# Hi/lo products of 384, 256 and 320 columns instead of three of 320, with a fold in PSUM, in a decoder layer on one core

## The chip, the cores and the metric

The kernel runs on one core of one Trainium2 chip. The metric is the device time of one execution in microseconds. Before the change it is 2016.62 us, the median of 3 runs (2016.05 to 2017.05). The numbers below come from one profiled execution of the kernel before, which took 2011.32 us itself.

## The reference

One decoder layer, 2048 channels wide, in float32, for a prompt of 256 tokens and for 8 sequences of 8 new tokens, which share all weights. Each token group has its own conditioning vector. Cut to what matters:

```python
mod = jax.nn.silu(c) @ w_ada + b_ada                    # six shifts, scales and gates
h = _rmsnorm(x, norm1_g) * (1 + sc1) + sh1
p = h @ w_in                                            # q, k, v, og, u, ga, gb, alr
o, s_new = _gla(q, k, v, loga, s0)                      # gated linear attention, 4 heads
y_a = _rmsnorm(o, gla_norm_g) * jax.nn.silu(og)
y_b = _pool(u_ext, pos0, w_pool, pool_scale)            # (window mean - u) @ w_pool, times a scale
merged = jax.nn.sigmoid(ga) * y_a + jax.nn.sigmoid(gb) * y_b
x = x + g1 * (merged @ w_o)
h2 = _rmsnorm(x, norm2_g) * (1 + sc2) + sh2
gate, up = jnp.split(h2 @ w_gu, 2, axis=-1)             # 2 x 5632 columns
x = x + g2 * ((jax.nn.silu(gate) * up) @ w_down)
y = _rmsnorm(x, final_norm_g)
```

Outputs are the normalised tokens of both groups and the new attention and pooling states.

## The kernel before, in words

Tokens are columns. Both groups lie side by side in tiles of T = 320 columns (256 of the prompt, 64 of the new tokens), with 128 channels on the partitions. So a projection has a piece of weights, 128 input by 128 output channels, as the stationary operand and 320 token columns as the moving one, and adds its result into one bank of PSUM.

Float32 accuracy is had from a split into a high and a low part in the type fp32r. Activations are split once when they are made: `hh` and `hl` (input of w_in), `mh` and `ml` (of w_o), `h2h` and `h2l` (gate and up), `ah` and `al` (down), `dh` and `dl` (of w_pool). Weights are split as they arrive: SyncE starts a transfer into a `raw` tile, ScalarE casts 512 columns of it to `whi` (L152), and VectorE subtracts to get `wlo` (L153); `whi` and `wlo` have five buffers each, and one holds two contraction tiles of 256 output channels. `mm3` (L165 to L168) then issues three products into the same columns of the bank: whi by high, whi by low, wlo by high. These three are called a triple in the following.

A unit is 256 output channels: a tile `ps` with two banks ([128, 2, 512], of which 320 columns in each are used), filled by all contraction tiles of the unit, each with two triples, one a bank. There are two `ps` buffers. When the unit is done, ScalarE or VectorE takes its result out (`evac`, the activation of gate, the product of up, or `residual`), and the buffer goes to the unit after the next.

The stages follow each other. In the head of the kernel the conditioning is worked out while w_in's first group of units runs in slices of the contraction: 2, 2, 4, 4 and 4 of the 16 contraction tiles, 15 units each time, with the partial results added in SBUF. In slices of two tiles a unit has only 12 products. Then come the units of heads 1 to 3 with all 16 tiles (96 products), between which the steps of the attention and pooling are taken from a queue; w_o in 8 units; the second norm; and the FFN in two parts, each of 22 units of gate and up and 8 units of down with 22 contraction tiles (132 products). Down's units end with `residual` (L999), as do w_o's.

What sets the order: the program is written engine by engine by a scheduler that simulates the work by estimated times; SyncE's weight transfers in the head are held in the written order. Each engine takes its instructions strictly in its own order, and waits on semaphores for the others. `xT`, the transposed input, lies in the tiles that later hold the low parts (tag `hl`), and is spilled to DRAM by POOL (L499) before these are written.

## Time and profile before

| | before |
|---|---|
| median of 3 runs | 2016.62 us (2016.05 to 2017.05) |
| profiled execution | 2011.32 us, span 2009.5 us |
| mean granted TensorE clock | 0.989 |
| matmuls, and weight loads | 15008 each |
| HBM read, written | 373.96 MB, 24.67 MB; 198 GB/s over the span |

The page gives for each engine its busy time, its share of the span, and its instructions. PE is TensorE's products and PEld its weight loads, which run beside them. A row of the groups reads: line, engine, operation, output tile <- input tiles, shapes, count; then busy us and mean ns of one; then the idle time of the engine just before, and what ended it. A shape such as 128*128 128x320 is a stationary operand of 128 rows by 128 columns and a moving one of 320 columns. A row of the timeline begins with the start and the length in us. A row of the waits reads: who waited, for whom, us in total, times, longest us. A row of the windows gives the length of the stretch, busy us and count of PE, PEld, VectorE, ScalarE and POOL, the granted clock, the transfers' busy share and GB/s.

### The profile page before, as it was taken

What the parts mean: (1) busy time and instruction counts of PE and PEld (TensorE: products, weight loads), DVE (VectorE), ACT (ScalarE), POOL (GpSimd) and SP (SyncE); (2) the same over time, 40 slices, a digit from 0 to 9 for tenths busy, and PEclk for the clock granted to TensorE, in tenths of its full rate; (3) what the DMA queues carried; (4) which work ended last, traced back from release to release, by engine and by line L of the source; (5) the groups of instructions that cost most, each with busy time, mean ns of one, the idle gap of its engine ahead of it and who ended that gap; (6) DMA issues with size and microseconds to landing.
All of it is one profiled execution on the core that took longest, in us unless ns stands there. A gap on an engine that the chain in (4) does not pass through costs nothing.

```text
span 2009.5 us, 37187 instructions
## 1 busy us (share of the span) xinstructions
PE 1956.2 (97%) x15008; PEld 1848.8 (92%) x15008; DVE 1015.5 (51%) x1881; ACT 820.1 (41%) x1466; POOL 141.8 (7%) x261
## 2 busy tenths in 40 slices
PE   7999999999999999999989999999999999999997
PEld 5789998888899899889979999999999999999997
DVE  3555665465546433665574444444444444444554
ACT  4333374354336333643344333343333344344443
POOL 1112220111001100110020000000000000000000
PEclk9999999999999999999989999999999999999998
DMA  9888754775975887569737666544444544444442
GB/s 301 285 302 272 234 155 147 253 255 186 314 237 167 281 263 229 156 230 340 234 105 223 206 205 203 168 148 154 145 152 149 155 149 147 151 154 144 150 142 91
DMA packets 319598, 400.83 MB, mean 199 GB/s; under 512 B 13529, under 2 KB 259801, under 8 KB 319089
## 3 DMA queue, kind: packets, MB, share of 16 engines
q1 hardware_dynamic: 307154, 358.21, 55.8%
q0 software_dynamic: 12272, 40.25, 5.7%
q8 instruction: 117, 1.92, 0.4%
q14 instruction: 55, 0.45, 0.1%
HBM read 373.96 MB, written 24.67 MB: 198 GB/s over the span
## 4 chain that ended last, share of the span: by engine, by line
PE 91%; DMA 5%; DVE 1%; ACT 1%; issue 1%; SPq 0%; POOL 0%; ACTq 0%; POOLq 0%; DVEq 0%
PE ps L166 27%; PE ps L168 26%; PE ps L167 26%; PE pm L218 5%; DMA raw<-w_in 2%; DMA raw<-w_ada 2%; PE pm L129 2%; PE pm L800 1%; PE pm L769 1%; PE pm L821 1%; DMA xn<-x_sample 1%; DVE wlo L153 0%; PE pm L796 0%; PE pm L758 0%; PE pm L641 0%
## 5 line engine op out<-in xcount | busy, mean ns | idle before, releaser
L153 DVE TENSOR_TENSOR wlo<-raw,whi 128x512 fp32r<-128x512 f32 x952 | 659.6, 697 | 834.0 <-ACT whi L152 827.2
L152 ACT CAST whi<-raw 128x512 fp32r<-128x512 f32 x952 | 587.0, 621 | 1013.4 <-PE ps L167 878.0
L166 PE MATMUL ps<-hh,whi 128*128 128x320 f32 x1408 | 445.9, 317 | 7.3 <-ACT whi L152 3.1
L166 PE MATMUL ps<-h2h,whi 128*128 128x320 f32 x1408 | 437.8, 311 | 5.1 <-ACT h2h L1042 5.1
L168 PE MATMUL ps<-hh,wlo 128*128 128x320 f32 x1408 | 441.6, 314 | 0.2 <-DVE wlo L153 0.2
L167 PE MATMUL ps<-hl,whi 128*128 128x320 f32 x1408 | 440.3, 313 | 0.3 <-DVE hl L495 0.3
L167 PE MATMUL ps<-h2l,whi 128*128 128x320 f32 x1408 | 435.5, 309 | 0.0
L168 PE MATMUL ps<-h2h,wlo 128*128 128x320 f32 x1408 | 435.5, 309 | 0.0
L166 PEld LDWEIGHTS ps<-hh,whi 128*128 128x128 f32 x1408 | 266.6, 189 | 30.8 <-issue 15.8
L168 PEld LDWEIGHTS ps<-hh,wlo 128*128 128x128 f32 x1408 | 266.6, 189 | 8.1 <-issue 6.1
L166 PEld LDWEIGHTS ps<-h2h,whi 128*128 128x128 f32 x1408 | 265.0, 188 | 9.3 <-ACT h2h L1042 6.1
L167 PEld LDWEIGHTS ps<-hl,whi 128*128 128x128 f32 x1408 | 266.9, 190 | 7.0 <-issue 5.4
L167 PEld LDWEIGHTS ps<-h2l,whi 128*128 128x128 f32 x1408 | 264.9, 188 | 0.0
L168 PEld LDWEIGHTS ps<-h2h,wlo 128*128 128x128 f32 x1408 | 264.9, 188 | 0.0
L166 PE MATMUL ps<-ah,whi 128*128 128x320 f32 x704 | 218.7, 311 | 0.0
L168 PE MATMUL ps<-ah,wlo 128*128 128x320 f32 x704 | 217.5, 309 | 0.0
L167 PE MATMUL ps<-al,whi 128*128 128x320 f32 x704 | 217.5, 309 | 0.0
L167 PEld LDWEIGHTS ps<-al,whi 128*128 128x128 f32 x704 | 132.2, 188 | 0.0
L166 PEld LDWEIGHTS ps<-ah,whi 128*128 128x128 f32 x704 | 132.2, 188 | 0.0
L168 PEld LDWEIGHTS ps<-ah,wlo 128*128 128x128 f32 x704 | 132.2, 188 | 0.0
L218 PE MATMUL pm<-raw,scT 128*32 128x128 f32 (+1 forms) x2688 | 109.9, 295 | 8.1 <-DMA raw<-w_ada 8.0
L218 PEld LDWEIGHTS pm<-raw,scT 128*32 128x32 f32 x2688 | 69.1, 111 | 36.0 <-issue 19.5
(279 smaller groups left out, 1542.6 us busy)
## 6 DMA issues: line engine op xcount, KB each, us to landing
raw<-w_ada SPq DMA_DIRECT2D x192, 512.0 KB, 5.8
raw<-w_gu SPq DMA_DIRECT2D x176, 512.0 KB, 3.5
raw<-w_in SPq DMA_DIRECT2D x173, 512.0 KB, 3.9
raw<-w_down SPq DMA_DIRECT2D x80, 512.0 KB, 3.3
S<-state_gla POOLq DMA_DIRECT2D x16, 1024.0 KB, 8.2
o_gs<-S POOLq DMA_DIRECT2D x16, 1024.0 KB, 5.9
raw<-w_o SPq DMA_DIRECT2D x32, 512.0 KB, 4.7
raw<-w_down SPq DMA_DIRECT2D x16, 256.0 KB, 2.6
```

Source lines behind the costliest of these rows:

```text
L129: PE.transpose(out, in_, ident[:k, :k])
L152: S.copy(hi, raw)
L153: V.tensor_sub(lo, raw, hi.bitcast(F32))
L166: PE.matmul(ps, lhsT=whi, rhs=xhi, start=start, stop=False)
L167: PE.matmul(ps, lhsT=whi, rhs=xlo, start=False, stop=False)
L168: PE.matmul(ps, lhsT=wlo, rhs=xhi, start=False, stop=stop)
L218: ins = PE.matmul(ps[32 * j:32 * j + 32, 0:w], lhsT=scT[:, k, :], rhs=raws[j], start=k == 0, stop=k == KT - 1, tile_position=(0, 32 * j))
L769: PE.matmul(pt, lhsT=E["kdn"][:, s, d * P:(d + 1) * P], rhs=E["vn"][:, s], start=s == 0, stop=s == 1)
L800: PE.matmul(pt[32 * j:32 * j + 32, :], lhsT=qeP[:, d, 4 * gg + j, :], rhs=E["S0", gg, d][:, j], start=False, stop=d == 1, tile_position=(0 ...
L821: PE.matmul(pt, lhsT=kpz[:, gg, j, d * P:(d + 1) * P], rhs=E["vp"][:, gg], start=True, stop=True)
```

## The change

High and low part of an activation now lie in one tile of 640 columns (`hx`, `mx`, `h2x`, `ax`, `dx`): 0 to 320 high, 320 to 640 low. A triple still covers 960 columns in three products, cut in other places (`EX` = 64):

- h: whi by columns 0 to 384, so all of the high part and the first 64 columns of the low part, into columns 0 to 384 of the bank;
- m: whi by columns 384 to 640, the other 256 of the low part, into columns 64 to 320;
- l: wlo by columns 0 to 320, as before, into columns 0 to 320.

What the first 64 low columns gave lies in columns 320 to 384 of the bank and belongs into 0 to 64. `fold` does this once a `ps` tile, before it is taken out: ScalarE copies the 64 columns of both banks to SBUF (one buffer), VectorE adds them into the bank. There are 180 such tiles: 75 in the head, 29 in heads 1 to 3, 8 of w_o, 44 of gate and up, 16 of down, and 8 of w_pool.

In the FFN's second part the products stand in another order: gate and up issue h, h, m, m, l, l over the two banks, down h, l, m for each bank. The padding tile `rpad` shrinks from 120 to 88 columns. `xT` now lies in the tile of both parts, so the high part too is written only after POOL's spill.

```diff
+EX = 64
-    rp.tile([P, 120], F32, name="rpad")
+    rp.tile([P, 88], F32, name="rpad")
...
-    def mm3(ps, whi, wlo, xhi, xlo, start, stop):
-        PE.matmul(ps, lhsT=whi, rhs=xhi, start=start, stop=False)
-        PE.matmul(ps, lhsT=whi, rhs=xlo, start=False, stop=False)
-        PE.matmul(ps, lhsT=wlo, rhs=xhi, start=False, stop=stop)
+    def halves(x):
+        return x[..., 0:T], x[..., T:2 * T]
+
+    def mm_pair(banks, ws, x, start, stop, order="hml"):
+        for part in order:
+            for ps, (whi, wlo) in zip(banks, ws):
+                if part == "h":
+                    PE.matmul(ps[:, 0:T + EX], lhsT=whi, rhs=x[:, 0:T + EX], start=start, stop=False)
+                else:
+                    o, w, rhs = (EX, whi, x[:, T + EX:2 * T]) if part == "m" else (0, wlo, x[:, 0:T])
+                    PE.matmul(ps[:, o:T], lhsT=w, rhs=rhs, start=False, stop=stop and part == order[-1])
+
+    def mm3(ps, whi, wlo, x, start, stop):
+        mm_pair([ps], [(whi, wlo)], x, start, stop)
+
+    def fold(ps):
+        t = wp.tile([P, 2, EX], F32, tag="fold", bufs=1, name=nm("fold"))
+        S.copy(t, ps[:, :, T:T + EX])
+        V.tensor_tensor(ps[:, :, 0:EX], ps[:, :, 0:EX], t, op=ALU.add)
+        return ps
...
-                for i in range(2):
-                    mm3(ps[:, i, :T], whi[:, i * P:(i + 1) * P], wlo[:, i * P:(i + 1) * P],
-                        xh[kt], xl[kt], kt == k0, kt == k1 - 1)
+                jobs = [(ps[:, i], (whi[:, i * P:(i + 1) * P], wlo[:, i * P:(i + 1) * P])) for i in range(2)]
+                for part in ([jobs] if both else [[b] for b in jobs]):
+                    mm_pair([b for b, _ in part], [w2 for _, w2 in part], x[kt], kt == k0, kt == k1 - 1, order)
             ada_pump()
-        return ps
+        return fold(ps)
...
-                xT.append(hp.tile([P, T], F32, tag="hl%d" % k, name="xT%d" % k))
+                xT.append(hp.tile([P, 2 * T], F32, tag="hx%d" % k, name="xT%d" % k)[:, 0:T])
...
-                pg = proj(wgu, f * P, 0, KT, h2h, h2l)
+                pg = proj(wgu, f * P, 0, KT, h2x, both=pi == 1)
...
-            ps = proj(wdn, 256 * ui, f0, f1, ah, al)
+            ps = proj(wdn, 256 * ui, f0, f1, ax, "hlm" if pi == 1 else "hml")
```

How this stands in the engines' orders is shown at three places. In a row stand the line, the operation, output <- inputs with their buffer numbers, and the shape of the moving operand or of the output.

TensorE, the down product of FFN part 2, before: the triple of one contraction tile in the second bank, and the next contraction tile's in the first bank (`ah` and `al` are the activations, `whi` and `wlo` the weights).

```order
L166 MATMUL ps_21143<-ah_18462,whi_21248 128x320
L167 MATMUL ps_21143<-al_18463,whi_21248 128x320
L168 MATMUL ps_21143<-ah_18462,wlo_21249 128x320
L166 MATMUL ps_21143<-ah_18743,whi_21264 128x320
L167 MATMUL ps_21143<-al_18744,whi_21264 128x320
L168 MATMUL ps_21143<-ah_18743,wlo_21265 128x320
```

The same place now, and below it two contraction tiles of gate and up in part 2, where "x2" is the same form twice, once for each bank:

```order
L176 MATMUL ps_21606<-ax_18885,whi_21711 128x384
L179 MATMUL ps_21606<-ax_18885,wlo_21712 128x320
L179 MATMUL ps_21606<-ax_18885,whi_21711 128x256
L176 MATMUL ps_21606<-ax_19171,whi_21727 128x384
L179 MATMUL ps_21606<-ax_19171,wlo_21728 128x320
L179 MATMUL ps_21606<-ax_19171,whi_21727 128x256
```

```order
L176 MATMUL ps_16887<-h2x_11666,whi_16974 128x384 x2
L179 MATMUL ps_16887<-h2x_11666,whi_16974 128x256 x2
L179 MATMUL ps_16887<-h2x_11666,wlo_16975 128x320 x2
L176 MATMUL ps_16887<-h2x_11667,whi_16974 128x384 x2
L179 MATMUL ps_16887<-h2x_11667,whi_16974 128x256 x2
L179 MATMUL ps_16887<-h2x_11667,wlo_16975 128x320 x2
```

The number of products is the same; their widths are 384, 320 and 256 or come in pairs over the banks.

VectorE in the head's first slice, before: subtractions for coming weights and the evacuations that fall to it.

```order
L153 TENSOR_TENSOR wlo_528<-raw_525,whi_527 128x512
L351 TENSOR_SCALAR v_281<-ps_460 128x640
L153 TENSOR_TENSOR wlo_532<-raw_525,whi_531 128x512
L340 COPY u_282<-ps_478 128x8x8 x2
L153 TENSOR_TENSOR wlo_586<-raw_583,whi_585 128x512
```

The same units on VectorE now:

```order
L188 TENSOR_TENSOR ps_376<-ps_376,fold_395 128x2x64
L188 TENSOR_TENSOR ps_399<-ps_399,fold_418 128x2x64
L188 TENSOR_TENSOR ps_436<-ps_436,fold_449 128x2x64
L154 TENSOR_TENSOR wlo_527<-raw_524,whi_526 128x512
L154 TENSOR_TENSOR wlo_531<-raw_524,whi_530 128x512
L188 TENSOR_TENSOR ps_453<-ps_453,fold_466 128x2x64
L371 TENSOR_SCALAR v_265<-ps_453 128x640
L188 TENSOR_TENSOR ps_474<-ps_474,fold_493 128x2x64
L360 COPY u_266<-ps_474 128x8x8 x2
```

VectorE now has an addition for every unit, also for those that ScalarE takes out, ahead of the coming weights' subtractions.

ScalarE in the same slice, before: casts of weights and its evacuations of q, k, the first half of v, and u.

```order
L152 CAST whi_481<-raw_479 128x512
L349 ACTIVATE q_279<-ps_392 128x640
L349 ACTIVATE k_280<-ps_412 128x640
L349 ACTIVATE v_281<-ps_446 128x640
L152 CAST whi_527<-raw_525 128x512
L152 CAST whi_531<-raw_525 128x512
L338 COPY u_282<-ps_478 128x2x256
```

The same now:

```order
L153 CAST whi_477<-raw_475 128x512
L187 COPY fold_395<-ps_376 128x128
L369 ACTIVATE q_263<-ps_376 128x640
L187 COPY fold_418<-ps_399 128x128
L369 ACTIVATE k_264<-ps_399 128x640
L187 COPY fold_449<-ps_436 128x128
L153 CAST whi_526<-raw_524 128x512
L153 CAST whi_530<-raw_524 128x512
L369 ACTIVATE v_265<-ps_436 128x640
L187 COPY fold_466<-ps_453 128x128
```

Each evacuation has a copy in front of it, and between the two lies VectorE's addition; the third unit's copy stands before two casts and its evacuation behind them. Over the whole program VectorE's order grows by the 180 additions, and ScalarE's by the 180 copies; SyncE has 708 transfers in both, some of w_ada, w_in and w_o in another order.

More of the change, by code (lines that the diff above doesn't have):

```diff
@@ L293, in s3 @@
         return ap.rearrange("p (b t) -> p b t", t=LS)
-    hh = [hp.tile([P, T], F32R, tag="hh%d" % k, name="hh%d" % k) for k in range(KT)]
-    hl = [None] * KT
+    hx = [None] * KT
     def hilo(hi, lo, x):
@@ L976, in body @@
     pump(len(queue))
[L979 to L980 removed]
+    mx = [hp.tile([P, 2 * T], F32R, tag="hx%d" % k, name="mx%d" % k) for k in range(KT)]
     for k in range(KT):
[L982 removed]
+        hilo(*halves(mx[k]), merged[k // 4][:, k % 4])
     mix.close()
@@ L1033, in body @@
     rs = rstd_bcast(acc)
-    h2h = [hp.tile([P, T], F32R, tag="hh%d" % k, name="h2h%d" % k) for k in range(KT)]
-    h2l = [hp.tile([P, T], F32R, tag="hl%d" % k, name="h2l%d" % k) for k in range(KT)]
+    h2x = [hp.tile([P, 2 * T], F32R, tag="hx%d" % k, name="h2x%d" % k) for k in range(KT)]
+    h2h, h2l = zip(*(halves(x) for x in h2x))
     for k in range(KT):
```

67 lines of the change are left out of this document (31 added, 36 removed).

## The prediction

> **What bounds the kernel now.** I read the page first (busy shares, then the chain that ended last), after it the groups by form, the matmuls' pitch in the timeline, and the list of waits.
>
> ```profile
> span 2009.5 us, 37187 instructions
> PE 1956.2 (97%) x15008; PEld 1848.8 (92%) x15008; DVE 1015.5 (51%) x1881; ACT 820.1 (41%) x1466; POOL 141.8 (7%) x261
> PE 91%; DMA 5%; DVE 1%; ACT 1%; issue 1%; SPq 0%; POOL 0%; ACTq 0%; POOLq 0%; DVEq 0%
> ```
>
> TensorE is busy for 97% of the span and carries 91% of the chain; VectorE (51%) and ScalarE (41%) have room. The work that the change reshapes is these groups, the first product of each three:
>
> ```profile
> L166 PE MATMUL ps<-hh,whi 128*128 128x320 f32 x1408 | 445.9, 317 | 7.3 <-ACT whi L152 3.1 <-ACT hh L491 2.7 <-DVE mg L927 0.6
> L166 PE MATMUL ps<-h2h,whi 128*128 128x320 f32 x1408 | 437.8, 311 | 5.1 <-ACT h2h L1042 5.1
> L166 PE MATMUL ps<-ah,whi 128*128 128x320 f32 x704 | 218.7, 311 | 0.0
> L166 PE MATMUL ps<-mh,whi 128*128 128x320 f32 x256 | 79.8, 313 | 0.0
> L166 PE MATMUL psy<-dh,whi 128*128 128x320 f32 x32 | 10.7, 336 | 3.4 <-ACT q L349 3.4
> ```
>
> 1408 + 1408 + 704 + 256 + 32 = 3808 triples. The 311 to 336 ns is the length of one, which overlaps its neighbours. What counts is the distance between starts:
>
> ```profile
> 1500.00:1600.00 100.00, 100.00 (x684) 100.00 (x683) 45.04 (x73) 38.36 (x62) 0.00 (x0) 1.00 0.48 150
> 1500.09 0.31 PE L166 MATMUL ps<-ah,whi 128*128 128x320 f32 x1
> 1500.23 0.31 PE L167 MATMUL ps<-al,whi 128*128 128x320 f32 x1
> 1500.38 0.31 PE L168 MATMUL ps<-ah,wlo 128*128 128x320 f32 x1
> 1500.53 0.31 PE L166 MATMUL ps<-ah,whi 128*128 128x320 f32 x1
> ```
>
> The first row is a stretch of 100 us in FFN part 1: 684 products, nothing idle, clock 1.00, so 100/684 = 0.146 us each and 0.44 us a triple, the same within a triple and from one to the next (0.14, 0.15, 0.15). 3808 x 0.44 = 1676 us of the span are these triples: 1 ns on a triple is 3.8 us. That decides the sign.
>
> **The triple: 384 + 256 + 320 columns for three of 320.** The sum stays 960 columns, the products three, the weight loads three. If a product costs so much a column and so much fixed, nothing moves. Other widths of the same kind are in the trace:
>
> ```profile
> 894.04 0.39 PE L821 MATMUL pm<-vp,kpz 128*128 128x512 f32 x1
> 894.27 0.31 PE L168 MATMUL psy<-dh,wlo 128*128 128x320 f32 x1
> 435.00 0.77 PE L640 MATMUL pm<-cumr,w 128*128 128x272 f32 x4
> 435.60 0.31 PE L166 MATMUL ps<-hh,whi 128*128 128x320 f32 x1
> L640 PE MATMUL pm<-cumr,w 128*128 128x400 f32 x8 | 3.1, 401 | 0.0
> L640 PE MATMUL pm<-cumr,w 128*128 128x272 f32 x8 | 2.6, 325 | 0.7 <-ACT w L627 0.7
> ```
>
> 512 columns hold TensorE 0.23 us, 320 hold it 0.146: 0.084/192 = 0.44 ns a column and 6 ns fixed by the rounded numbers; with 0.227, which rounds to the same 0.23, it is 0.417 ns a column and 13 ns fixed. On any such straight line a triple costs 0.44 us as before. The four products of L640 are 272, 400, 272 and 400 columns (the line's two forms, below them in the rows, as often as each other): 0.60 us, where the line gives 1344 x 0.417 + 4 x 13 = 613 ns. Uneven widths were thus not dearer here, but 13 ns cheaper for two pairs, with 10 ns of rounding. I take 0, by the straight line through the two widths with many rows; ends: -6.5 ns a triple (half of 13, a triple has one uneven pair) = -25 us, and the load's bound below for the other.
>
> **The weight load under 256 columns.** Each product needs a new load of 128 columns, which runs beside the product before it. The shortest cover falls from 320 columns (0.146) to 256, which the line puts at 0.120.
>
> ```profile
> L218 PEld LDWEIGHTS pm<-raw,scT 128*32 128x32 f32 x2688 | 69.1, 111 | 36.0 <-issue 19.5 <-DMA raw<-w_ada 11.3 <-DMA x<-xspill 0.4
> L512 PEld LDWEIGHTS pm<-hh,wal 128*64 128x64 f32 x16 | 2.2, 135 | 0.2
> L166 PEld LDWEIGHTS ps<-h2h,whi 128*128 128x128 f32 x1408 | 265.0, 188 | 9.3 <-ACT h2h L1042 6.1 <-issue 3.0 <-ACT h2h L1041 0.2
> ```
>
> From 64 to 128 columns a load grows by 53 ns, 0.83 a column, so 106 ns of the 188 is the part that grows and the rest passes in the pipe: an estimate that fits under 0.120. A second bound: in the 0.60 us of L640, the two products of 400 columns need at least 2 x 400 x 0.417 = 333 ns, which leaves at most 267 ns for the two of 272, 0.133 each, with loads of 128 columns under them. So a load never held TensorE longer than 133 ns there, and the 256-column product can be stretched by 13 ns at most: 3808 x 13 = +50 us. I take 0 here: 106 is nearer to what two sizes of load show. The Trainium skill ("TensorE: Matmul & The Clock Gate", section LDWEIGHTS) has a load take its columns over 1.2 ns, 107 ns for 128; the rows above agree by their slope. By that rule the sum is the same as by the rows, with 13 ns to spare; a load that also needed the fixed 13 ns to itself would just use it up.
>
> **Product orders in FFN part 2.** h, h, m, m, l, l over two banks, and h, l, m in the down product: no product more or less. In before, a product that reuses the weights' tile (L166 to L167), one that changes it (L167 to L168) and one that changes the bank (L168 to L166) all start 0.14 to 0.15 apart, so the order is worth 0.
>
> **The fold.** Columns 320 to 384 of a bank have to come back to 0 to 64: one ScalarE copy of 128 elements a partition out of PSUM and one VectorE add into it, per ps tile, 180 times, ahead of the evacuation.
>
> ```profile
> L1089 ACT COPY yn<-pm 128x128 f32<-128x128 f32 x16 | 4.2, 265 | 8.1 <-PE pm L129 8.1
> L1089 DVE COPY yn<-pm 128x128 f32<-128x128 f32 x16 | 4.7, 292 | 3.6 <-ACT yn L1089 3.5
> L1002 DVE TENSOR_TENSOR rt<-ps,mod 128x64 f32<-128x64 f32 x48 | 10.3, 215 | 0.0
> ```
>
> The copy is 0.27; the add of 128 elements lies between 0.22 (64 elements) and something over 0.29 (a copy of 128), I take 0.30; with a hand-over between engines of 0.05 at most (40.26 to 40.31 in the rows below) the chain is 0.6 us. 180 x 0.27 = 49 us more on ScalarE, 180 x 0.30 = 54 on VectorE: 869 and 1070 us of 2010, under 54%, so as work it is hidden under TensorE. What is not hidden is the delay of the evacuation, where TensorE waits for the bank. There are two ps buffers; a unit of 14 us and more (96 products and more at 0.146) covers it entirely: all FFN, w_o and the units of heads 1 to 3. It is short in the head's two slices of two contraction tiles, 30 units of 12 products (12 x 0.146 = 1.76 us). A unit's last product ends 0.3 after its start, the evacuation takes 0.7 to 0.8, and the buffer is wanted 13 x 0.146 = 1.9 after that start: cover 0.75, left after the fold about 0.15. But the units don't all begin evacuating at once:
>
> ```profile
> 39.56 0.70 ACT L349 ACTIVATE q<-ps 128x640 f32<-128x640 f32 x1 [3.36 <-PE ps L168]
> 40.31 0.41 PE L166 MATMUL ps<-hh,whi 128*128 128x320 f32 x1
> 115.74 0.82 DVE L347 SCALAR_TENSOR_TENSOR q<-ps,q 128x640 f32<-128x640 f32 x1
> 116.61 0.41 PE L166 MATMUL ps<-hh,whi 128*128 128x320 f32 x1 [0.22 <-DVE q L347]
> ```
>
> Here 40.31 follows the end of its evacuation (40.26) by 0.05, and 116.61 its own (116.56) by 0.05. These are the first and the last of ten such places among the 30 where less than 0.6 lies between; their mean is 0.25, so ten times 0.35 = +3.5 us. Ends: 0, since this stretch also waits for weights, and 30 x 0.6 = +18, if every unit pays in full.
>
> ```profile
> 0.00:200.00 200.00, 183.87 (x1519) 157.45 (x1520) 102.10 (x196) 70.49 (x129) 32.59 (x71) 0.99 0.87 290
> ACT whi L152 <- DMA raw<-w_in: 78.5, 21, 8.2
> PE psy L166 <- ACT q L349: 3.4, 1, 3.4
> PE ps L166 <- DVE mg L927: 0.6, 1, 0.6
> ```
>
> In the first 200 us the transfers are busy 0.87 of the time, and ScalarE waits 78.5 us for w_in: a late bank there can hide behind a late weight. In heads 1 to 3 two places wait for an evacuation or its follower (last two rows): 2 x 0.55 = +1.1, ends 0 and +1.2. The last two places are the ends of w_o and of the kernel, where the residual stands alone on the path:
>
> ```profile
> 1027.64 0.31 PE L168 MATMUL ps<-mh,wlo 128*128 128x320 f32 x1
> 1027.99 0.48 DVE L999 SCALAR_TENSOR_TENSOR x<-ps,mod,x 128x256 f32<-128x256 f32 x1 [0.56 <-PE ps L168]
> 1031.63 1.41 PE L1025 MATMUL pm<-acc,cst 128*128 128x320 f32 x2 [3.68 <-DVE acc L996]
> 1993.36 0.31 PE L168 MATMUL ps<-ah,wlo 128*128 128x320 f32 x1
> 1993.70 0.48 DVE L999 SCALAR_TENSOR_TENSOR x<-ps,mod,x 128x256 f32<-128x256 f32 x1 [7.60 <-PE ps L168]
> ```
>
> In both the fold stands between the last product and the first residual: +0.6 each; ends 0.3 and 0.6, the lower if the copy, whose columns only the h products write, starts under the last two products (2 x 0.146). In before, the first residual at 1027.99 reads only bank 0, complete three products earlier, and yet begins after the last product: so waits here are for the whole tile, and I take 0.6. The Trainium skill ("PSUM — Partial Sum Buffer", section PSUM bank collisions raise a hardware error) wants an engine kept off a bank that TensorE still writes; by that too the new orders buy nothing here and the sum is the same.
>
> Both added instructions also stand in queues. VectorE's add waits for the copy, and behind it on VectorE wait the wlo halves of coming weights; ScalarE's copy waits for the unit's last product, and behind it the whi halves. The five whi and wlo buffers hold ten contraction tiles of 6 x 0.146 = 0.88 us, so TensorE has up to 8.8 us in hand where the transfers are on time: 0, with the 18 above as its bound. The high part, now in the low part's tile, waits like it for POOL's spill of xT:
>
> ```profile
> L499 POOL DMA_DIRECT2D xspill<-xT x16: 542/542/622, 35.3 to 167.3; - x16
> 64.72 0.51 ACT L490 ACTIVATE hh<-xh,mod 128x256 fp32r<-128x256 f32 x1
> ```
>
> The first spills are issued from 35.3, the high parts that come into their tiles are written from 64.72: 29 us cover it, cost 0. SyncE has the same 708 transfers with a few swapped in order: 0, since TensorE's waits for them are in the head only.
>
> **Sum.** Triple 0, load 0, order 0, head +3.5, heads 1 to 3 +1.1, ends of w_o and kernel +1.2: +5.8 us on the profiled run's 2011.32 (span 2009.5). The median of the runs shown, 2016.62, lies 5.3 us above that run; the same difference on it gives **2022.4 us**, 0.29% slower. A measurement of this kernel can tell about 0.2%, 4.0 us, from no change.
>
> **The rivals.** (a) Faster: the uneven triple is cheaper. For it: the 13 ns of L640; against it: the rounding, and the straight line. Half of it, 3 ns a triple, gives -11.4 + 5.8 = -5.6: 2011.0. It decides from (4.0 + 5.8)/3808 = 2.6 ns a triple on; at 6.5 ns it is 2016.6 - 24.7 + 5.8 = 1997.7. (b) Slower by the load: it isn't covered by 256 columns and costs up to 13 ns a triple, 2016.6 + 5.8 + 50 = 2072; half of that, 2047. Against it: the slope of 0.83 ns a column. (c) Slower by the queues: every unit of the two short slices pays the whole fold and 18 us come in place of 3.5: 2037. For it: in-order queues with one fold buffer; against it: 20 of 30 units have the room, and the waits for weights hide part. (d) No change: the folds are all hidden or pressed under a measurement's uncertainty (the head's 3.5 gone behind weights): 2016.6 + 2.3 = 2019.
>
> **Chances.** The forecast with its folds' costs between 4 and 13: 0.43. (a) 0.27. (b) 0.09. (c) 0.06. (d) 0.15. So faster 0.27, same 0.15, slower 0.58. The range goes from 1998, the 6.5 ns end of (a), to 2037, the end of (c), and leaves out (b) and little of (a), 0.13 in all; the likeliest case's own range is 2020 to 2030.
>
> **What would show it.** In a dense stretch of the FFN a triple still takes 0.44 us, with 0.173, 0.120 and 0.146 for the three widths; a 256-column product at 0.13 would be (b), a triple under 0.437 (a). In the two short slices, waits of TensorE for ScalarE's or VectorE's evacuation grow by 2 to 5 us in sum; at the end of w_o the residual starts 0.9 after the last product instead of 0.35. I am wrong if the FFN's time per unit moves at all.

## The result, and the profile after

The changed kernel takes 2041.7 us (median of 4 runs, 2038.11 to 2042.34) against 2016.53 us of the kernel before in the same comparison: a ratio of 1.0121, 95% interval 1.0104 to 1.0139. It is slower by 25 us, where 6 were forecast. The profiled execution took 2038.11 us.

The page after, busy shares and the chain that ended last:

```profile
span 2036.3 us, 37600 instructions
PE 1965.3 (97%) x15008; PEld 1858.2 (91%) x15008; DVE 1061.3 (52%) x2061; ACT 852.0 (42%) x1645; POOL 137.4 (7%) x261
PE 87%; DMA 6%; DVE 3%; ACT 2%; issue 1%; POOL 0%; SPq 0%; ACTq 0%; DVEq 0%; POOLq 0%
```

The span is 26.8 us longer, and TensorE is busy for only 9 of them. The added work is no larger than forecast (VectorE +46 us where 54 were forecast, ScalarE +32 for 49), but VectorE and ScalarE have come into the chain: 3% and 2%, 1% each before.

To find where the time went, I compare when each stage's first product starts in the two traces. The stretches follow each other without a gap, so the differences add up to the span's, but for rounding:

| stretch | before, us | after, us | difference |
|---|---|---|---|
| up to w_in's first product | 34.6 | 35.8 | +1.2 |
| head, five slices of w_in | 266.2 | 283.6 | +17.4 |
| heads 1 to 3 | 597.6 | 600.4 | +2.8 |
| w_o and second norm | 139.8 | 138.2 | -1.6 |
| FFN part 1, gate and up | 331.2 | 333.6 | +2.3 |
| FFN part 1, down | 154.9 | 154.9 | 0.0 |
| FFN part 2, gate and up | 309.8 | 312.1 | +2.3 |
| FFN part 2, down | 159.3 | 160.4 | +1.1 |
| from the last product's start | 16.1 | 17.5 | +1.4 |

The head's row is the distance between these two products of the timeline, w_in's first and the first of head 1, before:

```profile
34.58 0.42 PE L166 MATMUL ps<-hh,whi 128*128 128x320 f32 x1 [2.68 <-ACT hh L491]
...
300.78 0.31 PE L166 MATMUL ps<-hh,whi 128*128 128x320 f32 x1
```

and after:

```profile
35.75 0.66 PE L176 MATMUL ps<-hx,whi 128*128 128x384 f32 x1 [3.48 <-DVE hx L514]
...
319.31 0.34 PE L176 MATMUL ps<-hx,whi 128*128 128x384 f32 x1
```

Of the head's 17.4 us, 9.7 are lost in the 30 units of the two-tile slices (w_in's first product to the first of the third slice: 74.5 us before, 84.2 after) and 7.7 in the 45 units of the four-tile slices: 3.4 in the first two of these, 4.2 in the last. The waits from 34 to 122 us, which take in the two-tile slices, show how. TensorE's waits for evacuations before:

```profile
PE ps L166 <- DVE v L351: 0.3, 1, 0.3
PE ps L166 <- DVE q L347: 0.2, 1, 0.2
```

and after, the three longest, with the waits of ScalarE and VectorE for the fold:

```profile
PE ps L176 <- DVE mg L367: 3.6, 3, 2.2
PE ps L176 <- DVE mg L371: 2.1, 2, 1.6
PE ps L176 <- DVE k L367: 2.0, 1, 2.0
...
ACT fold L187 <- PE ps L179: 32.2, 16, 3.7
DVE ps L188 <- ACT fold L187: 20.2, 13, 3.3
```

TensorE now waits 9.7 us for evacuations, three smaller rows included, which in this stretch of before cost it 0.5 us; for the weights' high halves it waits less than before (1.1 us instead of 3.1), and for low halves not at all, as before. ScalarE stands 32 us in front of fold copies whose unit isn't done, VectorE 20 us in front of additions whose copy isn't done; what is behind them in the two queues stands too. One such place in the timeline. The unit whose buffer is wanted ends with the product at 76.92, the next unit, in the other buffer, with the one at 78.67; the product at 82.00 gets the first one's buffer:

```profile
76.92 0.31 PE L179 MATMUL ps<-hx,wlo 128*128 128x320 f32 x1
78.67 0.31 PE L179 MATMUL ps<-hx,wlo 128*128 128x320 f32 x1
79.44 0.62 ACT L153 CAST whi<-raw 128x512 fp32r<-128x512 f32 x1 [3.84 <-DMA raw<-w_in]
79.97 0.26 ACT L187 COPY fold<-ps 128x128 f32<-128x128 f32 x1
80.09 0.69 DVE L154 TENSOR_TENSOR wlo<-raw,whi 128x512 fp32r<-128x512 f32 x1 [3.30 <-ACT whi L153]
80.70 0.29 DVE L188 TENSOR_TENSOR ps<-ps,fold 128x128 f32<-128x128 f32 x1
81.03 0.82 DVE L367 SCALAR_TENSOR_TENSOR k<-ps,k 128x640 f32<-128x640 f32 x1
82.00 0.42 PE L176 MATMUL ps<-hx,whi 128*128 128x384 f32 x1 [2.02 <-DVE k L367]
```

ScalarE had waited 3.84 us for a transfer of weights when the cast began at 79.44; both units' copies stand behind that cast, the second unit's not until 81.08; the first addition comes behind the subtraction that needs the cast, though its copy ended at 80.23, and the evacuation behind the addition. It ends at 81.85, 4.9 us after its unit's last product, and TensorE has waited 2.02 us. Over the 30 units the fold ends 1.67 us after the start of the unit's last product in the mean (0.94 would be the product and 0.6 us of fold), and 4.07 us at most. In the four-tile slices it is 2.0, 1.9 and 2.8.

Not all of the head's loss is a late bank. In the last slice TensorE's longest wait is for a step of the attention, `w`, which stands in the same queues. Before and after:

```profile
PE pm L641 <- DVE w L628: 1.4, 1, 1.4
PE pm L661 <- ACT w L648: 3.2, 1, 3.2
```

And the granted clock is lower. From 34 to 122 us, before and after (the share behind POOL's):

```profile
34.00:122.00 88.00, 83.12 (x711) 72.62 (x712) 50.01 (x93) 32.44 (x62) 16.41 (x34) 0.98 0.88 304
34.00:122.00 88.00, 75.46 (x634) 64.89 (x635) 53.93 (x116) 35.67 (x88) 15.35 (x34) 0.96 0.84 290
```

Besides a stretch at w_in's first product, which both have, the head of before shows a clock of 0.50 for 3.41 us from 280.63; after, it is 0.50 for 3.41 us from 83.27 and for 6.83 us from 291.48, each beside a wait of TensorE (2.02 and 3.2 us). Since 6.83 us more run at half the clock, I estimate up to 3.4 of the 17.4 us as this second price of the waits. Other waits, such as one of 2.15 us at 116, are not followed by it; what decides is not settled here.

The FFN's triples. The count of products in the same 260 us of gate and up in part 2, and in 100 us of part 1's down, before:

```profile
1560.00:1820.00 260.00, 260.00 (x1775) 260.00 (x1774) 115.69 (x166) 103.48 (x166) 0.00 (x0) 1.00 0.49 150
1400.00:1500.00 100.00, 100.00 (x684) 100.00 (x683) 46.06 (x87) 35.06 (x58) 0.00 (x0) 1.00 0.48 153
```

and after:

```profile
1560.00:1820.00 260.00, 260.00 (x1761) 260.00 (x1760) 120.11 (x183) 106.97 (x185) 0.00 (x0) 1.00 0.47 148
1400.00:1500.00 100.00, 100.00 (x684) 100.00 (x684) 46.89 (x92) 36.18 (x62) 0.00 (x0) 1.00 0.45 150
```

In part 1's down, 384 + 256 + 320 columns take exactly what three of 320 take. In part 2's gate and up, 1761 products against 1775 make a triple 0.8% longer: 443.3 ns by the starts in the trace, 440.0 before. The clock is 1.00 in all four rows.

The tail, where the fold stands alone on the path:

```profile
2018.81 0.28 PE L179 MATMUL ps<-ax,whi 128*128 128x256 f32 x1
2019.42 0.30 DVE L188 TENSOR_TENSOR ps<-ps,fold 128x128 f32<-128x128 f32 x1 [7.84 <-ACT fold L187]
2019.76 0.48 DVE L1017 SCALAR_TENSOR_TENSOR x<-ps,mod,x 128x256 f32<-128x256 f32 x1
```

The residual starts 0.95 after the last product, 0.34 before: the fold's 0.6. Of the row's other 0.8 us the trace shows that the clock of 0.50, at which the last small products run in both kernels, begins 3.2 us after the last product instead of 4.2.

At the end of w_o, where the prediction expected the same 0.6, work for the coming weights stands ahead of both halves of the fold:

```profile
1047.14 0.31 PE L179 MATMUL ps<-mx,wlo 128*128 128x320 f32 x1
1047.35 0.62 ACT L153 CAST whi<-raw 128x512 fp32r<-128x512 f32 x1 [1.13 <-PE ps L179]
1047.87 0.26 ACT L187 COPY fold<-ps 128x128 f32<-128x128 f32 x1
1047.99 0.69 DVE L154 TENSOR_TENSOR wlo<-raw,whi 128x512 fp32r<-128x512 f32 x1 [1.05 <-ACT whi L153]
1048.61 0.29 DVE L188 TENSOR_TENSOR ps<-ps,fold 128x128 f32<-128x128 f32 x1
1048.93 0.48 DVE L1017 SCALAR_TENSOR_TENSOR x<-ps,mod,x 128x256 f32<-128x256 f32 x1
```

Here the residual starts 1.79 after the last product instead of 0.35: the same fold of 0.6 us costs 1.4 where it has to stand behind a cast and a subtraction. Little of it reaches TensorE, since gate and up's first product comes 10.7 us after w_o's last one, 10.5 before.

### The profile page after: what moved, and what is told of

It is laid out like the page before. It is cut to its first block, busy times and chain, and to the rows that moved or that the text cites. A ratio compares the mean times of both kernels' runs of the same rounds, so it can differ in the third digit from the quotient of the medians.

```text
span 2036.3 us, 37600 instructions
## 1 busy us (share of the span) xinstructions
PE 1965.3 (97%) x15008; PEld 1858.2 (91%) x15008; DVE 1061.3 (52%) x2061; ACT 852.0 (42%) x1645; POOL 137.4 (7%) x261
## 4 chain that ended last, share of the span: by engine, by line
PE 87%; DMA 6%; DVE 3%; ACT 2%; issue 1%; POOL 0%; SPq 0%; ACTq 0%; DVEq 0%; POOLq 0%
PE ps L179 46%; PE ps L176 31%; PE pm L239 4%; DMA raw<-w_in 3%; DMA raw<-w_ada 2%; PE pm L130 2%; DVE wlo L154 1%; PE pm L821 1%; PE pm L842 1%; ACT whi L153 1%; PE pm L790 1%; DMA xn<-x_sample 1%; PE pm L817 0%; PE pm L779 0%; DVE S L844 0%
## 5 line engine op out<-in xcount | busy, mean ns | idle before, releaser
L176 PE MATMUL ps<-hx,whi 128*128 128x384 f32 x1408 | 487.8, 347 | 18.1 <-DVE mg L367 4.8
L179 PE MATMUL ps<-hx,wlo 128*128 128x320 f32 x1408 | 440.1, 313 | 0.2 <-DVE wlo L154 0.2
L176 PE MATMUL ps<-h2x,whi 128*128 128x384 f32 x1408 | 423.2, 341 | 5.1 <-DVE h2x L1061 5.1
L179 PE MATMUL ps<-hx,whi 128*128 128x256 f32 x1408 | 401.7, 285 | 0.0
L179 PE MATMUL ps<-h2x,wlo 128*128 128x320 f32 x1408 | 380.0, 311 | 0.0
L179 PE MATMUL ps<-h2x,whi 128*128 128x256 f32 x1408 | 339.8, 282 | 0.0
L176 PEld LDWEIGHTS ps<-hx,whi 128*128 128x128 f32 x1408 | 267.3, 190 | 41.7 <-issue 17.5
L179 PEld LDWEIGHTS ps<-hx,wlo 128*128 128x128 f32 x1408 | 266.8, 190 | 9.3 <-issue 7.4
L179 PEld LDWEIGHTS ps<-hx,whi 128*128 128x128 f32 x1408 | 266.7, 189 | 7.1 <-issue 6.5
L179 PEld LDWEIGHTS ps<-h2x,whi 128*128 128x128 f32 x1408 | 262.3, 189 | 0.0
L176 PEld LDWEIGHTS ps<-h2x,whi 128*128 128x128 f32 x1408 | 251.5, 189 | 8.8 <-ACT h2x L1060 5.6
L179 PEld LDWEIGHTS ps<-ax,whi 128*128 128x128 f32 x704 | 132.3, 188 | 0.0
L176 PEld LDWEIGHTS ps<-ax,whi 128*128 128x128 f32 x704 | 132.2, 188 | 0.0
```

Source lines behind the costliest of these rows:

```text
L176: PE.matmul(ps[:, 0:T + EX], lhsT=whi, rhs=x[:, 0:T + EX], start=start, stop=False)
L179: PE.matmul(ps[:, o:T], lhsT=w, rhs=rhs, start=False, stop=stop and part == order[-1])
```

## The experiments

Each kernel's ratio is against the kernel before on the same chip (medians there 2010.5 to 2012.4 us; the three kernels with other paddings ran once each, beside one run of before, 2018.66). Each trace is of one execution, and the scheduler orders each kernel anew, so two of them can differ by that too. "Head" is the distance from w_in's first product to head 1's first product, 266.2 us in before's trace and 283.6 in the changed kernel's. Triples are worked out from the starts of six consecutive products, as means over the places of a stage where no other product stands between.

### Without the fold

```diff
     def fold(ps):
-        t = wp.tile([P, 2, EX], F32, tag="fold", bufs=1, name=nm("fold"))
-        S.copy(t, ps[:, :, T:T + EX])
-        V.tensor_tensor(ps[:, :, 0:EX], ps[:, :, 0:EX], t, op=ALU.add)
         return ps
```

> The changed kernel without the fold: columns 320 to 384 are never added back, so the first 64 token columns lack the low part's share. Theory (the fold, standing in ScalarE's and VectorE's queues, holds the banks back): of the 25 us the orders' 3.4 us in FFN part 2 stay and most of the rest goes, about 2020 to 2023, and in the head's slices of two contraction tiles TensorE's loss against before falls from 10 us to under 2. Rival (the tile of 640 columns and the order that the scheduler makes of it cost the time): it stays above 2035.

Measured: 2024.13 us, ratio 1.005 (1.0034 to 1.0066). The head:

```profile
35.62 0.98 PE L176 MATMUL ps<-hx,whi 128*128 128x384 f32 x2 [3.48 <-DVE hx L511]
...
300.80 0.34 PE L176 MATMUL ps<-hx,whi 128*128 128x384 f32 x1
```

265.2 us: all 17.4 us are gone, with the tile of 640 columns, the widths and the orders still in place. What stays are the FFN's longer triples (gate and up 442.3 and 443.3 ns in the two parts, part 2's down 444.5), 5.4 us by the stages. But this is the trace of the fastest of six executions (2017.43 us). The median lies 11.7 us above before's, where I had expected 3.5 to 6.5, and the other 6 us are in no trace. The traced execution had a granted clock of 0.991, the others 0.987 to 0.990; before's had 0.987 to 0.991.

### A fold of zeros in the kernel before

```diff
+    def fold(ps):
+        t = wp.tile([P, 2, 64], F32, tag="fold", bufs=1, name=nm("fold"))
+        S.activation(t, ps[:, :, 0:64], AF.Copy, scale=0.0)
+        V.tensor_tensor(ps[:, :, 0:64], ps[:, :, 0:64], t, op=ALU.add)
+        return ps
...
-        return ps
+        return fold(ps)
```

(in the three helpers that fill ps tiles, and for w_pool; `rpad` has 88 columns, as in the changed kernel)

> The kernel before with a fold of zeros in every ps tile: ScalarE writes 64 columns of both banks times zero to SBUF, VectorE adds them; products, widths and tiles as before. Theory (fold in the queues): about 2034 to 2038, with 10 us or so lost in the two short slices. Rival (layout): no more than my 5.8 us, up to 2023.

Measured: 2030.87 us, ratio 1.0095 (1.0074 to 1.0115). The head:

```profile
35.92 0.56 PE L166 MATMUL ps<-hh,whi 128*128 128x320 f32 x2 [2.68 <-ACT hh L498]
...
318.88 0.31 PE L166 MATMUL ps<-hh,whi 128*128 128x320 f32 x1
```

283.0 us, 16.8 more than before, and 440.0 ns a triple in the FFN. The fold with its place in the orders makes the head's loss without the uneven products, and none of the FFN's. The total, 18 us above the 2012.42 us of before here, is at the lower edge of what I expected (18 to 22 above 2016.5); from the changed kernel's ratio it differs by 0.0026, some 5 us, which is about the FFN's share.

### The orders undone in FFN part 2

```diff
-                pg = proj(wgu, f * P, 0, KT, h2x, both=pi == 1)
+                pg = proj(wgu, f * P, 0, KT, h2x, both=False)
...
-            ps = proj(wdn, 256 * ui, f0, f1, ax, "hlm" if pi == 1 else "hml")
+            ps = proj(wdn, 256 * ui, f0, f1, ax, "hml")
```

> The changed kernel with h, m, l for each bank in FFN part 2 too. Theory (a triple costs 440.0 ns in the order h, m, l, as in part 1's down product, and 443 in the new orders): part 2 is 3.4 us shorter, about 2038. Rival (the 3.4 us are the fold's, at the units' ends): no change in part 2, 2041 to 2042.

Measured: 2042.99 us, ratio 1.0137 (1.0111 to 1.0164). Neither theory: down in part 2 went back to 440.0 ns, but gate and up, in the order h, m, l of part 1, got slower:

```profile
1560.00:1820.00 260.00, 260.00 (x1748) 260.00 (x1747) 119.08 (x181) 105.65 (x182) 0.00 (x0) 1.00 0.49 148
```

1748 products in the 260 us, 446.7 ns a triple. The same three widths in the same order take 440.0 ns in down and 446.7 in gate and up. My reading of the changed trace ("the order costs 3 ns") was wrong.

### No uneven products and no fold in the head

```diff
     def proj(w, col, k0, k1, x, order="hml", both=False):
+        ex = EX if k1 - k0 == KT or k1 - k0 == 22 else 0
...
-        return fold(ps)
+        return fold(ps) if ex else ps
```

(the rest of the edit hands `ex` to the products, and sets it to 0 in the paired units of the head)

> The changed kernel with three products of 320 columns and no fold in the head's five slices (75 units); everything else as changed. Theory (fold in the queues, dear where units are short): the 14 us that the slices lost against before come back, 2024 to 2028. Rival (layout, and the spill that the high part now waits for): the head stays long, above 2037.

Measured: 2015.86 us, ratio 1.0017 (1.0005 to 1.003). The head takes 265.5 us. More came back than expected: with the 105 folds of the longer units left in, the end of w_o's products comes 2.5 us ahead of before's. Where a unit has 96 products and more, the fold is hidden as far as the stages show, as forecast.

### The fold on VectorE alone

```diff
-        S.copy(t, ps[:, :, T:T + EX])
+        V.tensor_copy(t, ps[:, :, T:T + EX])
```

> The changed kernel with the fold's copy on VectorE instead of ScalarE: no hand-over, and no copy in ScalarE's queue, where in the changed kernel it stands behind casts that wait for weights. Theory A (the queues: a fold waits behind casts on ScalarE and behind wlo on VectorE): the loss up to the end of the head's slices, 17 us in the changed kernel's trace, falls to 8 to 12, the kernel to 2028 to 2034 by the runs of before here. Theory B (the chain's own length of 0.6 us per unit): still 15 to 18 us, since 0.29 and 0.30 on one engine are as long.

Measured: 2066.16 us, ratio 1.0269 (1.0243 to 1.0295): the slowest of all. The head takes 291.4 us, 25 more than before, and heads 1 to 3 lose too. Theory A, which expected 8 to 12 us in the head, falls: the copy's place behind ScalarE's casts is not by itself the trouble. The waits from 34 to 122 us:

```profile
DVE fold L187 <- PE ps L179: 13.8, 10, 3.1
DVE wlo L154 <- ACT whi L153: 9.5, 10, 2.9
```

Now VectorE itself stands in front of units that aren't done, and the additions and evacuations stand behind that, with the weights' low halves. TensorE's own waits in this stretch name VectorE's evacuations (8.0 us) and no low half. Theory B's 15 to 18 us are exceeded as well: in the two-tile slices the loss is about the same (9.9 us), but the last slice takes 77.2 us instead of 64.9, with a granted clock of 0.91 there (0.97 before).

### Three ps buffers, changed kernel and before

```diff
-    pmain = ctx.enter_context(tc.tile_pool(name="pmain", bufs=2, space=PSUM))
-    pmisc = ctx.enter_context(tc.tile_pool(name="pmisc", bufs=4, space=PSUM))
+    pmain = ctx.enter_context(tc.tile_pool(name="pmain", bufs=3, space=PSUM))
+    pmisc = ctx.enter_context(tc.tile_pool(name="pmisc", bufs=2, space=PSUM))
```

> The changed kernel with three ps buffers and two small PSUM tiles instead of two and four: a bank may be held one unit (1.76 us in the two-tile slices) longer. Theories A and B (the bank is given back too late): of the 10 us lost in the two-tile slices under 2 stay; what two small tiles cost elsewhere is shown by the next run. Rival C (the added work on ScalarE and VectorE makes the weights' halves late): the 10 us stay.

> The kernel before with three ps buffers and two small PSUM tiles, as the control of the run ahead: the ten tight places in the two-tile slices get room, so 0 to 3 us less there; heads 1 to 3, which use the small tiles, may lose. Between 2008 and 2025.

Measured: the changed kernel 2025.8 us, ratio 1.0069 (1.005 to 1.0087); before 2013.25 us, ratio 1.001 (0.9997 to 1.0023). With three buffers the head takes 264.4 us in the changed kernel and 258.5 in the kernel before: the fold's price falls from 17.4 to 5.9. Not all of these 11.5 us were late banks. The last slice gives 4.5 of them: it takes 57.8 and 58.1 us in these two kernels, whose orders have no wait for `w` there. What the third buffer can be credited with is 4.4 of the 9.7 us of the two-tile slices and 2.5 of the 3.4 of the next two, so 6.9 of 17.4. In the two-tile slices 5.3 us stay, more than the 2 I allowed. TensorE's longest waits up to 122 us, in the changed kernel and then in the kernel before:

```profile
PE ps L176 <- DVE hx L516: 4.6, 2, 3.8
PE ps L176 <- ACT q L369: 3.6, 1, 3.6
PE ps L176 <- ACT whi L153: 3.6, 3, 1.6
```

```profile
PE ps L166 <- ACT hh L491: 4.3, 1, 4.3
PE ps L166 <- ACT whi L152: 3.3, 2, 1.8
PE ps L166 <- ACT k L349: 0.9, 1, 0.9
```

The waits for activations and for weights' high halves are nearly the same in both. What is left of the difference is one evacuation by ScalarE (3.6 us against 0.9) and a second stretch of 3.41 us at a clock of 0.50, from 50.62, which before with three buffers doesn't have (1.7 us).

### The work without the delay

```diff
     def evac(ps, g, kind, i, acc):
+        evac_(ps, g, kind, i, acc)
+        if acc is not None:
+            work(g.u[:, :, PB:PB + 64] if kind == "u" else getattr(g, kind)[:, 2 * i:2 * i + 2, 0:64])
...
+    def work(x):
+        t = wp.tile([P, 2, 64], F32, tag="fold", bufs=1, name=nm("fold"))
+        S.copy(t, x)
+        V.tensor_tensor(t, t, t, op=ALU.add)
```

> The kernel before with the fold's work but not its delay, in the head's 75 units: behind each evacuation ScalarE copies 128 elements a partition out of SBUF and VectorE adds them into a scratch tile; no bank waits for it. Theories A and B (the bank is late): no more than 3 us up to the end of the head's slices. Rival C (the work itself): 10 us and more, as with the fold of zeros (17).

Measured: 2018.69 us, ratio 1.0031 (1.0019 to 1.0042). The head takes 271.8 us, 5.6 more than before: 1.7 in the two-tile slices, 0.4 less in the next two, and 4.3 in the last. The 1.7 are a stretch of 3.41 us at a clock of 0.50 (from 91.92); for evacuations TensorE waits 0.5 us there, as in before. So of the 13.1 us that the changed kernel loses in the first four slices, all but 1.3 need the delay of the bank, as theories A and B say. The last slice is as long as in the changed kernel (69.2 and 69.1 us), with the same wait for `w` (3.6 us) and the same 6.83 us at half clock: there the added work, with the order that the scheduler makes of it, is enough, as rival C says. That 5.6 is near the 5.9 us that three buffers left is chance: those lie in the two-tile slices.

### The layout and the orders with three products of 320

```diff
-EX = 64
+EX = 0
```

with an empty `fold`; in the second of the two kernels the orders of before too.

> The changed kernel with EX = 0: one tile of 640 columns, three products of 320, no fold, but FFN part 2 in the new orders (h, h, m, m, l, l and h, l, m). Theory D (the uneven widths stretch the triple, the order only together with them): 440.0 ns a triple in part 2, as before. Rival E (the order by itself): 443 ns in part 2, 3.4 us.

> As the run ahead, with the orders of before too: of the change only the layout in one tile is left, with the high part waiting for the spill. The layout should cost 0: within 4 us of before, and under 2 us of difference at the end of the head's slices. A rival that puts part of the head's 17 us on the layout expects 3 us and more there.

Measured: with the new orders 2013.73 us, ratio 1.0013 (1.0001 to 1.0025), without them 2014.02, ratio 1.0011 (1.0 to 1.0023). The head takes 266.6 and 266.1 us, gate and up in part 2 440.0 ns a triple in both. With the new orders:

```profile
1560.00:1820.00 260.00, 260.00 (x1775) 260.00 (x1774) 115.69 (x166) 103.64 (x167) 0.00 (x0) 1.00 0.49 150
```

The layout and the later high part cost nothing in the head, and the orders nothing by themselves. Theory D holds as far as the uneven widths are needed for the longer triple.

### Uneven products only in heads 1 to 3, w_o and w_pool

```diff
-        ex = EX if k1 - k0 == KT or k1 - k0 == 22 else 0
+        ex = EX if k1 - k0 == KT and x is not h2x else 0
```

(on top of the kernel with 320 in the head; the paired units of the FFN's start and both orders as before)

> Products of 384, 256 and 320 and the fold only where the trace showed them harmless: heads 1 to 3, w_o and w_pool; the head's slices and the FFN with 320. By the stages of the run without them in the head (2.5 us ahead of before at the end of w_o) and of before in the FFN: 2 us less than before, which is no difference that can be told; more than 4 us less would make the uneven widths worth having there.

Measured: 2008.82 us, ratio 0.9986 (0.9974 to 0.9997). As expected: 2.5 us less, about the smallest difference that can be told.

### A smaller unevenness

```diff
-EX = 64
+EX = 32
```

(on the kernel with 320 in the head, orders of before)

> EX = 32 instead of 64, so products of 352, 288 and 320, orders of before everywhere, none of it in the head's slices. If the stretched triple (446.7 ns in part 2's gate and up with 384, 256, 320 in the order h, m, l) comes from how uneven the widths are, it lies between 440 and 446.7 here; if it comes with any uneven cut, it is 446.7; by the straight line it is 440.0.

Measured: 2025.86 us, ratio 1.0075 (1.005 to 1.0101). Gate and up in part 2:

```profile
1560.00:1820.00 260.00, 260.00 (x1748) 260.00 (x1747) 118.47 (x182) 103.65 (x182) 0.00 (x0) 1.00 0.48 148
```

446.7 ns with 352, 288 and 320 columns, as with 384, 256 and 320; 440.0 in down. It comes with either uneven cut, and not with the size of the cut. Gate and up and down differ in several things; the next runs try one of them, where their activations lie.

### Other addresses for gate and up's activations

```diff
-    rp.tile([P, 88], F32, name="rpad")
+    rp.tile([P, 80], F32, name="rpad")
```

(80, 72 or 56 columns, on the kernel with 320 in the head and orders of before)

> The changed kernel without the fold in the head, orders of before everywhere, and the padding tile rpad of 80 columns instead of 88: gate and up's activation tiles lie 32 bytes elsewhere, down's stay. Theory F (where the moving operand lies sets how long an uneven triple takes): gate and up in part 2, 446.7 ns with 88 columns, moves to another value, towards 440 or below, and down stays at 440.0. Rival G (the address plays no part): 446.7 again.

> The same with rpad of 72 columns, 64 bytes from where it was. Theory F: a value other than 446.7 in gate and up at one of the three paddings at least. Rival G: 446.7.

> The same with rpad of 56 columns, 128 bytes from where it was. Theory F: as above. Rival G: 446.7.

Measured: 2012.4, 2010.8 and 2013.24 us in one run each, beside 2018.66 of before. Gate and up in part 2 with 80 columns:

```profile
1560.00:1820.00 260.00, 260.00 (x1775) 260.00 (x1775) 121.09 (x184) 106.43 (x184) 0.00 (x0) 1.00 0.49 150
```

440.0 ns in the mean at each of the three paddings, and 440.0 in down. With 88 columns the comparison is the run with the orders undone: 446.7 ns, and TensorE's products stand in the same order in part 2 there. Theory F holds in this stage: with the same products in the same order, the place of the moving operand decides between 440.0 and 446.7 ns. The padding of 88 columns was the only bad one of the four tried. The times of single runs can't be compared to a few us.

### The changed kernel at another address

```diff
-    rp.tile([P, 88], F32, name="rpad")
+    rp.tile([P, 72], F32, name="rpad")
```

> The changed kernel whole, but for rpad of 72 columns. Theory F: gate and up fall to 440.0 ns a triple in part 1 and in part 2, where the order is still h, h, m, m, l, l; the kernel gains 4 to 6 us, and 19 to 21 us above before stay, the fold's. Rival G': the new orders keep 443 by themselves: 2 us are gained.

Measured: 2028.73 us, ratio 1.0086 (1.0068 to 1.0103), 7 us (0.35%) nearer to before than the changed kernel. The instructions of every engine stand in the same order in both traces. The head is as long as in the changed kernel (282.6 us). Gate and up in part 1 (order h, m, l) falls to 440.0 ns. Part 2, in the order h, h, m, m, l, l:

```profile
1560.00:1820.00 260.00, 260.00 (x1801) 260.00 (x1801) 122.50 (x187) 108.88 (x189) 0.00 (x0) 1.00 0.50 152
```

1801 products, 433.4 ns a triple: faster than any triple of the kernel before. I had not expected that from either theory. Down's h, l, m, whose tiles this padding doesn't move, is at 442.6 (443.2 in the changed kernel).

### Two versions that the runs point to

The uneven products in heads 1 to 3, w_o and w_pool alone, with the padding of 72 columns:

```diff
-    rp.tile([P, 88], F32, name="rpad")
+    rp.tile([P, 72], F32, name="rpad")
```

> Uneven products and the fold in heads 1 to 3, w_o and w_pool only, with rpad of 72 columns: the triples there take 440.0 ns by theory F, where they took 440.5 in the mean with 88. That is under 1 us: 0.1 to 0.3% below before. If uneven widths had a gain of their own, it would have shown as triples under 440.

Measured: 2007.58 us, ratio 0.9989 (0.9977 to 1.0002): no difference that can be told. The triples there take 440.0.

And the pair order h, h, m, m, l, l in all units of 16 contraction tiles but the first two of the FFN, down in the order h, m, l, with 320 and no fold in the head:

```diff
-    rp.tile([P, 88], F32, name="rpad")
+    rp.tile([P, 72], F32, name="rpad")
...
+        both = k1 - k0 == KT
```

> The version that the runs point to: rpad of 72 columns, products of 384, 256 and 320 in the order h, h, m, m, l, l in heads 1 to 3, w_o and all of gate and up, in the order h, m, l in down, no fold and three products of 320 in the head's slices. If the pair order at this address takes 433.3 ns a triple, as it did in part 2's gate and up of the run ahead, heads 1 to 3 (928 triples), w_o (256) and gate and up (1376 of 1408) gain 6.7 ns each, 17 us: near 1993 on a chip where before takes 2011. If 433.3 holds only where nothing stands between the products (part 2), 4.7 us: 2003 to 2006.

Measured: 2007.36 us (12 runs), ratio 0.9981 (0.9967 to 0.9994). It is faster than the changed kernel and 0.19% faster than before, with an interval that just keeps off 1. Part 2's gate and up has its 433.4 ns again:

```profile
1560.00:1820.00 260.00, 260.00 (x1802) 260.00 (x1801) 122.50 (x188) 108.82 (x188) 0.00 (x0) 1.00 0.49 152
```

Elsewhere the pair order gives less: 435.5 in heads 1 to 3 and 438.1 in w_o and in part 1's gate and up in the mean, a mixture from 433 to 442. So the second of the two expectations is the nearer one. From these triples I estimate a gain of some 10 us, of which 3 show; the runs had a granted clock of 0.986 to 0.990, before's 0.988 to 0.992, which would account for some 4 us by another estimate; no run follows it up.

## Why the prediction was wrong

- **The step that failed** is the one on the queues: "TensorE has up to 8.8 us in hand where the transfers are on time: 0, with the 18 above as its bound". It asked what stands behind the fold, the weights' halves, and found them covered. So they were: TensorE's waits for high halves fell from 3.1 to 1.1 us. What cost time is the other direction: copy and addition stand behind casts and subtractions for coming weights, the evacuation stands behind the addition, and there TensorE has one unit in hand, 1.76 us and not 8.8. Its waits for evacuations grew from 0.5 to 9.7 us where 2 to 5 more were forecast. Measured for the head: 17.4 us in place of 3.5, 16.8 with a fold in the kernel before, none in the trace without it.
- That late transfers stretch the queues is read from places such as the one at 79.44 and from the prediction's own 78.5 us of waits for w_in; no run had the weights on time, so this part is argued and not shown.
- **Rival (c)** had the right reason, in-order queues, at a chance of 0.06. That its 18 us lie so near 17.4 is luck: they were 30 units times 0.6, and those 30 units lost 9.7.
- **The head's +3.5** counted, from the trace of before, ten of thirty places with too little room and gave each 0.35 us. That counting takes the fold as 0.6 us long wherever it stands. It ended 1.67 us after the last product's start in the mean, and with 0.76 of evacuation that is 2.4 us against the 1.9 after which TensorE wants the buffer: 0.5 us short on average over thirty units, 16 us, of which 9.7 showed, some of them as a lower clock. The four-tile slices, which the prediction left out, lost 7.7 us more.
- **How the loss splits.** First four slices, 13.1 us: 1.3 come with the work alone, the rest only when the bank waits for it; a third buffer gives back 6.9. Last slice, 4.2 us: the work alone loses as much, in a longer wait for `w` and at a clock of 0.50. Of the 17.4 us, up to 3.4 (an estimate) are the lower clock, for which the prediction had no term. That it is ScalarE's queue in particular was my theory A, and it fell.
- **Triple: 0** was right for the sum of widths (440.0 in part 1's down, and in the order h, m, l at three of four paddings) and missed what the place of the operand does: +2.3 us in each part's gate and up, and +1.1 in down with its new order. Within the bounds given, but not by the mechanism that set them; neither rival (a) nor (b) has it. By the prediction's own sign, "I am wrong if the FFN's time per unit moves at all", this too was a miss.
- **Load under 256 columns: 0** was right: the 256-column product takes 117 ns in part 1's down, as the straight line's 120 says, and no load was seen to hold it.
- **Orders: 0** was right for even widths (440.0 with the new orders and 320) and wrong for uneven ones: 443.3 at one address and 433.4 at another. The prediction's rows, in which every change of bank or weights costs nothing, were of equal products only.
- **Ends of w_o and the kernel: +0.6 each.** Right in the tail (0.95 instead of 0.34). At the end of w_o the residual came at 1.79 and not at the 0.9 forecast, for the reason that failed in the head; TensorE lost only 0.2 us there. **Heads 1 to 3: +1.1** measured +2.8, and 0.3 less than before with the fold alone; where it comes from is open. **Fold hidden in the long units**: right by the stages of the kernel with the fold only there (ratio 1.0017, part of which is the address).
- **Signs and size.** The sign was forecast with 0.58; the time, 2041.7, lies 5 us above the range's end at 2037, which held 18 us for the queues but none for the FFN's 5.7.

## What to carry to other kernels

An instruction added in front of an evacuation is priced by what stands ahead of it in its queue, not by its length: look where the two queues already stand for transfers, and where a unit is shorter than the wait plus the evacuation. There, leave the short units as they are and change the long ones only. When product widths are cut unevenly, measure the distance of starts at two or three paddings before judging the widths.

## What was not expected of the hardware

- The distance between starts depends on where the moving operand lies in SBUF. In part 2's gate and up, with products of 384, 256 and 320 columns in the order h, m, l, a triple takes 446.7 ns with the padding of 88 columns and 440.0 with 80, 72 or 56; in the order h, h, m, m, l, l, 443.3 with 88 and 433.4 with 72. Three products of 320 took 440.0 in every kernel that has them in the FFN, whichever the padding (120, 88 or 72). The clock was 1.00 in all these stretches.
- In heads 1 to 3 and part 1, where other products stand in between, the changed kernel shows 436.7 in some stretches and 446.7 in others, kept for many triples at a time, although the activations lie in the same tiles as in part 2. So the place is not the only thing that counts. What fixes which one a stretch falls into isn't settled, nor which address is good: four paddings were tried, and down's tiles were not moved at all.
